# A fast matrix product with seven multiplications: the fourth product accumulates on the bank of the first, sixth and seventh

## The chip, the core and the metric

The kernel runs on one core of one Trainium2 chip. The core has a matmul engine (PE, with its weight loads shown apart as PEld), a vector engine (DVE), a scalar engine (ACT), a general engine (POOL) and a queue engine (SP) that issues most DMAs. [...] The metric is device time in microseconds: the median of several executions.

## The reference

One layer: a norm, one wide projection, two groups of attention heads, and an output projection.

```python
h = rms_norm(x, pre_g)
z = jnp.einsum('bsd,de->bse', h, w_in)
qa, ka, va, ga, qb, kb, vb, gb, gk_low = split_columns(z)
...
oa = diff_attention(qa, ka, va, lam)          # 8 heads, two softmax maps each
oa = rms_norm(oa, subln_g) * (1.0 - lam_init) * silu(ga)
...
ob = gla_chunked(qb, kb, vb, log_a)           # 4 heads of gated linear attention
ob = rms_norm(ob, gla_g) * silu(gb)
y = jnp.einsum('bse,ed->bsd', jnp.concatenate([oa, ob], axis=-1), w_out)
return x + rms_norm(y, post_g)
```

The sequence and the model width are both 1024. `z` has 7184 columns. The change concerns the product of `h` (1024 x 1024) and `w_in`.

## The kernel before

**Split numbers.** Every 32-bit number is split into a high part in a matmul format and a low part, the rest. A product a x b is made of three matmul passes: high x high, high x low, low x high. An operand therefore costs an ACT cast for the high part and a DVE subtraction for the low part. For the weights these are lines 315 and 316.

**Seven products for eight.** The columns of `w_in` are taken 256 at a time: a *pair* of 128-column blocks. For each pair the 2 x 2 block product of the input (halves of the sequence by halves of the model width) and the weights (halves of the width by the two column blocks) is made by Winograd's form of Strassen's method. With h11, h12, h21, h22 the blocks of the input, and b11 to b22 those of the weights:

- s1 = h21 + h22, s2 = s1 - h11, s3 = h11 - h21, s4 = h12 - s2
- T1 = b12 - b11, T2 = b22 - T1, T3 = b22 - b12, T4 = b21 - T2
- product 1: h11 b11; 2: h12 b21; 3: s4 b22; 4: h22 T4; 5: s1 T1; 6: s2 T2; 7: s3 T3
- result (0,0) = 1 + 2; (0,1) = 1 + 6 + 5 + 3; (1,0) = 1 + 6 + 7 + 4; (1,1) = 1 + 6 + 7 + 5

(The fourth product's sign follows from how T4 is formed.) There are 28 pairs. Eight of them, the values of the two attention groups (kinds VB and VA), are *wide*: two of them are joined to a group of 512 columns, their weights are the moving operand, and a product has 24 matmuls of 256 columns. The other 20 are single; a product has 12 matmuls of 512 columns.

**Order.** `order` (lines 200 to 221) is the list of (pair, product), 196 in all. The first ten entries are first and second products of pairs 0 to 4, which only need the first half of the sequence. PE runs the matmuls in exactly the order of the program (`mm` keeps program order); the instructions of DVE, ACT and most of SP are ordered by the program's planner when it is built, by readiness and the order of writing. `go(n)` makes n steps; each step prepares the weights up to three entries ahead (`prepare`, `make_weights`) and then does `step(i)`.

**Banks.** `take_bank` hands out the eight PSUM banks in turn from a list of free ones. In `step`, products 1, 6 and 7 accumulate on bank x, 5 and 3 on bank z, 2 on bank y, and 4 on another bank named y. `snap` copies x to SBUF on ACT after products 1, 6 and 7 (s1, s2, s3, line 427). `done` (line 436) adds a bank and a snapshot on DVE (line 440, for wide pairs lines 403 and 411) and hands the sum to `take` or `take_values`, which scale, gate or split it and store it to DRAM through SP.

**Weights.** The raw halves of `w_in` come into four buffers with the tag raw (`load_raw`, line 194), which `fetch_raw` asks for at certain products. `make_weights` forms T1 to T4 in place in those buffers on DVE (line 296, one difference at each of products 5, 6, 4 and 7), casts them on ACT and makes the low part on DVE, into a ring of five tiles.

**Input blocks.** `blocks(j)` (lines 550 to 571) makes piece j of four of h22, s1, s2 and s3 from the second half of the sequence, by PE transposes, ACT and DVE; it runs between the first ten products. s4 follows in lines 623 to 627.

**Around it.** `wo_step` (line 580) splits `w_out` on the side: it opens a load of one 128 x 512 tile at products 2 and 4 and casts, subtracts and stores it at products 1 and 6. `low_rank` and `decay` make the gates of the linear attention between the projections; from pair 12 on, `gla` puts its matmuls between the products. The last eight entries of `order` (`LEAD`) run after the first loads of the attention, mixed with loads of the split `w_out` (`weights`, line 900) into the places of the input blocks that are no longer needed; the stores of these last steps keep the program's order on SP. Behind the projections come the attention of eight heads, and the output projection, `ypart` and `yps`.

Of the kernel before, what the change touches and what calls it, by code (L numbers as in the profile page):

```python
# [31 lines left out]
def hymba_kernel(  # L32
# [188 lines left out]
    order += [(y, 7), (z, 4), (z, 7), (y, 3), (z, 3)]  # L221
# [28 lines left out]
    def fetch_raw(p, n, i):  # L250

        if not wide(p):
            load_raw(p)
            if i >= n_early:
                load_raw(p + 1)
        elif p >= 4 or p == 0:
# [4 lines left out]
            if n == 4:  # L261
                load_raw(p + 2, (0,))
                if p == 0:
                    load_raw(3, (0,))
            elif n == 7:
                if p == 0:
                    load_raw(3, (1,))
                else:
                    load_raw(p + 2, (1,))
        else:  # L270
            if n == 5:
                load_raw(2, (1,))
            elif n == 4:
                load_raw(4, (0,))
            elif n == 7:
                load_raw(4, (1,))

    def make_weights(i):
# [6 lines left out]
        else:  # L285
# [13 lines left out]
            if n == 5:  # L299
# [3 lines left out]
            elif n == 4:  # L303
                src = sub(b21, b21, b11)
            elif n == 7:
                src = sub(b12, b22, b12)
            else:
                src = {1: b11, 2: b21, 3: b22}[n]
# [40 lines left out]
    def take(kind, n, half, unit, c):  # L349

        cs = cols(half)
        if kind in ("QA", "KA"):
# [3 lines left out]
            if ending and order[made[0] - 1][1] == 7:  # L356
# [5 lines left out]
            act.activation(hi, c, AF.Copy, scale=scale)  # L362
            dve.scalar_tensor_tensor(lo, c, scale, fp(hi), ALU.mult, ALU.subtract)
# [6 lines left out]
        elif kind in ("GA", "GB"):  # L370
            g = t_st("g")
            act.activation(g, c, AF.Exp, scale=-1.0)
            act.activation(g, g, AF.Ln, bias=1.0)
            act.activation(g, g, AF.Exp, scale=-1.0)
            dve.tensor_tensor(c, c, g, ALU.mult)
            d = g_d[n + unit] if kind == "GA" else gg_d[n][unit]
            sp.dma_start(d[:, cs], c)
        elif kind == "QB":
# [3 lines left out]
            dve.scalar_tensor_tensor(c, c, QSCALE, e_q[:, cs], ALU.mult, ALU.mult)  # L382
# [8 lines left out]
        else:  # L391
            g = n + unit
            dve.tensor_tensor(c, c, decs[g][1][:, cs], ALU.mult)
            sp.dma_start(gq_d[g][2, :, cs], c)

    def take_values(p, half, unit, p0, p1):
# [1128 lines left out]
```

## Time and profile before

| what | us |
|---|---|
| median of three runs | 982.13 |
| lowest and highest of them | 981.99, 982.59 |
| the profiled execution's own time | 980.34 |
| its span, first to last instruction | 978.6 |
| granted PE clock over the span | 0.999 |
| first matmul of a projection starts | 13.96 |
| last projection ends, first output matmul starts | 630.80 |

Rows of groups read: line of the kernel, engine, operation, output <- inputs by the program's names, count; then times. In a list in order of time the first two numbers are the start and the length in us, and in brackets stands how long the engine had been idle and what ended that. Rows of stretches give the length, then the busy time of PE, PEld, DVE, ACT and POOL, the granted clock, the DMA share and GB/s. Rows of waits give who waited for whom, the total, how many times, and the longest.

### The profile page before, as it was taken

The page shows a single profiled execution, that of the slowest core. Times are in us where ns is not written, and L with a number is a line of the kernel's source. Part 1 is how long each engine was busy: PE and PEld are TensorE (multiplying, and loading weights), DVE is VectorE, ACT ScalarE, POOL GpSimd, SP SyncE. Part 2 cuts the span into 40 slices and gives each one's busy share as a digit, 9 for nine tenths or more (in the row PEclk, how much of TensorE's full clock was granted, in tenths as well). Part 3 has the DMA queues.
Part 4 walks back from the last instruction along what each step waited for, and adds up shares of the span by engine and source line. Part 5 has one row for each costly group of instructions (what it writes and reads, how often), then busy time and mean ns, then how long its engine had stood idle before and what let it go on. Part 6 is the DMA issues. An engine that isn't in the chain of part 4 may idle for free.

```text
span 978.6 us, 15745 instructions
## 1 busy us (share of the span) xinstructions
PE 956.6 (98%) x5338; PEld 829.7 (85%) x5338; DVE 736.0 (75%) x1452; ACT 600.9 (61%) x1164; POOL 135.3 (14%) x142
## 2 busy tenths in 40 slices
PE   6999999999999999999999999999999999999997
PEld 5998988888889998899888888878888888888785
DVE  6986597798766677586786876487888888898554
ACT  8642365486467445445566765366777687887773
POOL 4300000000000010000100100021322222443322
PEclk9999999999999999999999999999999999999999
DMA  9443456646765858897988866997657669994777
GB/s 353 143 123 93 124 148 202 229 169 233 253 234 168 266 183 276 247 299 230 298 254 255 270 191 217 357 300 250 206 173 234 233 202 351 351 283 107 151 209 146
DMA packets 152593, 220.45 MB, mean 225 GB/s; under 512 B 17104, under 2 KB 83664, under 8 KB 152416
## 3 DMA queue, kind: packets, MB, share of 16 engines
q1 hardware_dynamic: 148480, 212.10, 66.5%
q0 software_dynamic: 4032, 7.34, 4.8%
q8 instruction: 42, 0.69, 0.3%
q14 instruction: 39, 0.32, 0.1%
HBM read 133.93 MB, written 88.60 MB: 227 GB/s over the span
## 4 chain that ended last, share of the span: by engine, by line
PE 87%; DMA 4%; DVE 4%; ACT 2%; issue 1%; SPq 1%; POOL 0%; DVEq 0%; ACTq 0%; POOLq 0%
PE x L117 21%; PE y L117 14%; PE z L117 14%; PE ypart L117 13%; PE sc L117 7%; PE po L117 5%; PE yps L117 4%; PE wtr L120 3%; PE gpo L117 2%; DMA ks<-k_d 1%; PE kv L117 1%; DMA wo_raw<-in_w_out_dram 1%; DMA w_raw<-in_w_in_dram 1%; PE gkl_ps L117 1%; DVE w L316 1%
## 5 line engine op out<-in xcount | busy, mean ns | idle before, releaser
L315 ACT CAST w<-w_raw 128x512 fp32r<-128x512 f32 (+1 forms) x164 | 112.4, 688 | 97.2 <-PE y L117 46.2
L316 DVE TENSOR_TENSOR w<-w_raw,w 128x512 fp32r<-128x512 f32 (+1 forms) x164 | 126.5, 773 | 52.1 <-ACT w L315 45.6
L1048 ACT ACTIVATE p<-p,stt 128x896 f32<-128x896 f32 (+7 forms) x128 | 99.3, 777 | 37.7 <-DVE stt L1038 33.6
L427 ACT COPY s<-x 128x512 f32<-128x512 f32 x84 | 49.1, 585 | 86.9 <-PE x L117 83.9
L1054 POOL TENSOR_SCALAR p<-p,stt,lam 128x1024 f32<-128x1024 f32 (+3 forms) x64 | 56.2, 877 | 226.2 <-DVE stt L1053 223.8
L296 DVE TENSOR_TENSOR w_raw<-w_raw 128x512 f32<-128x512 f32 (+1 forms) x96 | 75.8, 790 | 15.4 <-DMA w_raw<-in_w_in_dram 14.1
L1038 DVE CUSTOM_DVE_ANT_0 p<-sc,maskt 128x512 f32<-128x512 f32 (+3 forms) x128 | 74.3, 585 | 14.9 <-PE sc L117 13.8
L775 POOL TENSOR_SCALAR_AFFINE_SELECT gan<-gan 128x512 f32<-128x512 f32 x8 | 17.6, 2198 | 486.3 <-ACT gan L774 486.3
L117 PE MATMUL ypart<-wo_hi,m_hi 128*128 128x512 f32 x192 | 79.6, 414 | 0.1
L117 PE MATMUL y<-h_hi,w 128*128 128x512 f32 x320 | 79.6, 391 | 0.0
L117 PE MATMUL z<-s_hi,w 128*128 128x512 f32 x320 | 79.6, 391 | 0.0
L117 PE MATMUL x<-s_hi,w 128*128 128x512 f32 x320 | 79.6, 391 | 0.0
L117 PE MATMUL ypart<-wo_hi,m_lo 128*128 128x512 f32 x192 | 75.5, 393 | 0.0
L117 PE MATMUL ypart<-wo_lo,m_hi 128*128 128x512 f32 x192 | 75.4, 393 | 0.0
L117 PE MATMUL sc<-k,q 128*128 128x512 f32 (+1 forms) x192 | 69.0, 363 | 1.2 <-DVE stt L1038 1.2
L117 PEld LDWEIGHTS x<-s_hi,w 128*128 128x128 f32 x320 | 59.7, 188 | 12.2
L117 PEld LDWEIGHTS y<-h_hi,w 128*128 128x128 f32 x320 | 59.6, 188 | 12.2
L117 PEld LDWEIGHTS z<-s_hi,w 128*128 128x128 f32 x320 | 59.5, 188 | 12.0
L117 PE MATMUL sc<-ks,q 128*128 128x512 f32 (+1 forms) x192 | 66.1, 347 | 1.0 <-DMA ks<-k_d 1.0
L1096 ACT CAST wt_hi<-wtr 128x512 fp32r<-128x512 f32 (+1 forms) x80 | 42.8, 535 | 25.3 <-PE wtr L120 24.5
L1097 DVE TENSOR_TENSOR wt_lo<-wtr,wt_hi 128x512 fp32r<-128x512 f32 (+1 forms) x80 | 50.6, 633 | 9.1 <-ACT wt_hi L1096 8.5
L1057 DVE SCALAR_TENSOR_TENSOR p<-p,stt,p 128x1024 f32<-128x1024 f32 (+3 forms) x64 | 52.1, 814 | 4.1 <-POOL p L1054 3.9
(224 smaller groups left out, 2237.3 us busy)
## 6 DMA issues: line engine op xcount, KB each, us to landing
w_raw<-in_w_in_dram SPq DMA_DIRECT2D x56, 512.0 KB, 4.5
wo_raw<-in_w_out_dram SPq DMA_DIRECT2D x32, 256.0 KB, 2.8
wo_d<-wo_hi SPq DMA_DIRECT2D x32, 256.0 KB, 2.9
wo_d<-wo_raw SPq DMA_DIRECT2D x32, 256.0 KB, 3.3
q<-q_d SPq DMA_DIRECT2D x32, 256.0 KB, 4.6
k<-k_d SPq DMA_DIRECT2D x32, 256.0 KB, 5.3
ks<-k_d SPq DMA_DIRECT2D x64, 128.0 KB, 6.5
wo_hi<-wo_d SPq DMA_DIRECT2D x16, 512.0 KB, 6.4
```

Source lines behind the costliest of these rows:

```text
L117: tc.keep_in_program_order(pe.matmul(*a, **k))
L120: tc.keep_in_program_order(pe.transpose(dst, src, ident))
L296: dve.tensor_tensor(dst, a, b, ALU.subtract)
L315: act.copy(w[0], src)
L316: dve.tensor_tensor(w[1], src, fp(w[0]), ALU.subtract)
L427: act.copy(b[k], ps)
L1038: ins = dve.tensor_tensor_reduce(p[:, a:e], sc[:, : e - a], maskt[:, NZ + P - (e - a) :] if last else maskt[:, : e - a], 1.0, 3e38 if i == ...
L1048: act.activation(p[:, :n], p[:, :n], AF.Exp, bias=st[:, m : m + 1], scale=-1.0, accum_out=st[:, 2 + m : 3 + m],)
L1054: pool.tensor_scalar(p1[:, :n], p1[:, :n], st[:, 5:6], lam, ALU.mult, ALU.mult)
L1057: dve.scalar_tensor_tensor(p0[:, :n], p0[:, :n], st[:, 4:5], p1[:, :n], ALU.mult, ALU.subtract)
L1096: act.copy(hi[:, :n], pt[:, :n])
L1097: dve.tensor_tensor(lo[:, :n], pt[:, :n], fp(hi[:, :n]), ALU.subtract)
```

## The change

Product 4 no longer takes a bank: it accumulates on x behind products 1, 6 and 7, so that the result (1,0) stands complete in PSUM, and `done` hands the bank itself on without an add. The order of a pair becomes 1, 2, 6, 5, 7, the next pair's 1, 4, 3 (for a wide group 1, 2, 6, 5, 7, 4, 3, each for both of its pairs). The swap of two entries by hand is gone. The weights' sums are formed in another order: at product 6 T3 (in b12) and T2 (in b11), at product 5 T4 (in b21) and T1, none at 7 and 4; the last two pairs keep the old way, and their order gets 7 ahead of 4. The loads of raw weights and the steps of `w_out` hang on other products.

```diff
-    for prev, group in zip([[]] + groups, groups):
-        for n in (1, 2, 5, 6, 4, 7):
-            if (group[0], n) not in order[:n_early]:
-                order += [(p, n) for p in group]
-
-            if n == (7 - len(group) if group[0] < EARLY else 2):
-                order += [(p, 3) for p in prev]
-
-    i = order.index((1, 4))
-    order[i : i + 2] = order[i + 1], order[i]
-
-    order += [(y, 1), (y, 2), (y - 1, 3), (y, 5), (z, 1), (z, 2), (z, 5), (y, 6), (z, 6), (y, 4)]
-    order += [(y, 7), (z, 4), (z, 7), (y, 3), (z, 3)]
+    for group, after in zip(groups, groups[1:] + [[y]]):
+        for n in (1, 2, 6, 5, 7, 4, 3):
+            order += [(p, n) for p in group if (p, n) not in order]
+
+            if n == 7 and len(group) == 1:
+                order += [(p, 1) for p in after[:1]]
+
+    order += [(y, 2), (y, 5), (z, 1), (z, 2), (z, 5), (y, 6), (z, 6), (y, 7)]
+    order += [(z, 7), (y, 4), (z, 4), (y, 3), (z, 3)]
...
-            if i >= n_early:
+            if i >= n_early and n > 1:
                 load_raw(p + 1)
...
-            if n == 4:
+            if n == 7:
                 load_raw(p + 2, (0,))
+            elif n == 4:
                 if p == 0:
-                    load_raw(3, (0,))
-            elif n == 7:
-                if p == 0:
-                    load_raw(3, (1,))
+                    load_raw(3)
                 else:
                     load_raw(p + 2, (1,))
         else:
-            if n == 5:
+            if n == 6:
                 load_raw(2, (1,))
+            elif n == 7:
+                load_raw(4, (0,))
             elif n == 4:
-                load_raw(4, (0,))
-            elif n == 7:
                 load_raw(4, (1,))
...
-            if n == 5:
+            if n == 5 and p < y:
+                sub(b21, b21, b11)
+                src = sub(b11, b22, b11)
+            elif n == 6 and p < y:
+                sub(b12, b22, b12)
+                dve.tensor_tensor(b11, b11, b12, ALU.add)
+                src = b11
+            elif n == 5:
                 src = sub(b11, b12, b11)
...
-    def take(kind, n, half, unit, c):
+    def take(kind, n, half, unit, src, c):
...
-            act.activation(hi, c, AF.Copy, scale=scale)
-            dve.scalar_tensor_tensor(lo, c, scale, fp(hi), ALU.mult, ALU.subtract)
+            act.activation(hi, src, AF.Copy, scale=scale)
+            dve.scalar_tensor_tensor(lo, src, scale, fp(hi), ALU.mult, ALU.subtract)
...
-            dve.tensor_tensor(st, p0, p1, ALU.add)
+            if p1 is None:
+                act.copy(st, p0)
+            else:
+                dve.tensor_tensor(st, p0, p1, ALU.add)
...
-        name = {1: "x", 2: "y", 5: "z", 6: "x", 4: "y", 7: "x", 3: "z"}[n]
-        if n in (1, 2, 4, 5):
+        name = {1: "x", 2: "y", 5: "z", 6: "x", 4: "x", 7: "x", 3: "z"}[n]
+        if n in (1, 2, 5):
             b[name], b["i" + name] = take_bank([P, 512], name)
         ps = b[name]
-        multiply(i, ps, n not in (6, 7, 3))
-
-        def done(half, unit, p0, p1):
+        multiply(i, ps, n in (1, 2, 5))
+
+        def done(half, unit, p0, p1=None):
             if wide(p):
                 return take_values(p, half, unit, p0, p1)
             c = t_c("c")
-            dve.tensor_tensor(c, p0, p1, ALU.add)
-            take(kind, m, half, unit, c)
+            if p1 is not None:
+                dve.tensor_tensor(c, p0, p1, ALU.add)
+                p0 = c
+            take(kind, m, half, unit, p0, c)
...
         elif n == 7:
             snap("s3", ps)
+            done(1, 1, b["z"], b["s3"])
+        elif n == 4:
+            done(1, 0, ps)
             free.append(b["ix"])
-            done(1, 1, b["z"], b["s3"])
-            done(1, 0, b["y"], b["s3"])
-            free.append(b["iy"])
...
-        if n in (1, 6) and wo_open:
+        if n in (3, 6) and wo_open:
...
-        if n in (2, 4) and wo_todo:
+        if n in (2, 7) and wo_todo:
...
     go(2)
     mix0 = mix(0)
-    go(3)
+    go(4)
     weights(E + 6)
     weights(E + 7)
-    go(3)
+    go(2)
```

More of the change, by code (lines that the diff above doesn't have):

```diff
@@ L355, in take @@
             ending = made[0] > len(order) - LEAD
[L356 removed]
+            if ending and order[made[0] - 1][1] in (7, 4):
                 raw = ap.tile([P, 2, 512], F32R, tag="raw", name="qk_st", bufs=4)
@@ L439, in done @@
             c = t_c("c")
-            dve.tensor_tensor(c, p0, p1, ALU.add)
-            take(kind, m, half, unit, c)
+            if p1 is not None:
+                dve.tensor_tensor(c, p0, p1, ALU.add)
+                p0 = c
+            take(kind, m, half, unit, p0, c)
         if n == 1:
```

24 lines of the change are left out of this document (13 added, 11 removed).

## The prediction

> **What bounds the kernel now.** I read the page's head and its chain of waits first, then the stage table, then the waits of the matmul engine.
>
> ```profile
> span 978.6 us, 15745 instructions
> PE 956.6 (98%) x5338; PEld 829.7 (85%) x5338; DVE 736.0 (75%) x1452; ACT 600.9 (61%) x1164; POOL 135.3 (14%) x142
> PE 87%; DMA 4%; DVE 4%; ACT 2%; issue 1%; SPq 1%; POOL 0%; DVEq 0%; ACTq 0%; POOLq 0%
> ```
>
> PE holds 87% of the chain, so only what PE waits for is worth anything. The stages (length, then PE, weight load, DVE, ACT, POOL busy):
>
> ```profile
> 20.00:64.00 44.00, 42.57 (x334) 41.12 (x333) 42.63 (x66) 30.20 (x51) 9.87 (x10) 1.00 0.50 162
> 126.00:308.00 182.00, 182.00 (x833) 151.77 (x832) 144.20 (x235) 106.17 (x182) 0.66 (x1) 1.00 0.65 211
> 308.00:478.00 170.00, 169.18 (x1187) 158.15 (x1186) 121.74 (x181) 91.28 (x156) 10.99 (x5) 1.00 0.79 247
> 478.00:609.00 131.00, 131.00 (x651) 111.08 (x651) 96.48 (x155) 83.79 (x152) 5.93 (x2) 1.00 0.76 239
> 631.00:664.00 33.00, 30.66 (x147) 24.50 (x146) 25.75 (x78) 18.32 (x42) 6.62 (x8) 1.00 0.95 308
> ```
>
> The seven-product projections run from about 14 to 631 us. From 126 to 308 and from 478 to 609 PE has no idle time at all, and DVE, the engine that the change relieves, has slack. Only 20 to 64 is different: there DVE is busy 42.63 of 44 us. What PE waits for in the whole run:
>
> ```profile
> PE xT L120 <- DVE x L482: 8.9, 4, 7.2
> PE y L117 <- DVE s L565: 1.3, 1, 1.3
> PE sc L117 <- DMA ks<-k_d: 1.0, 1, 1.0
> PE y L117 <- ACT s L427: 0.7, 1, 0.7
> PE gpo L117 <- DVE gu L803: 0.5, 1, 0.5
> PE kv L117 <- DVE c L411: 0.3, 1, 0.3
> ```
>
> Apart from the first 14 us, which the change doesn't touch, the ceiling of any gain in the projections and just behind them is 1.3 + 1.0 + 0.7 + 0.5 + 0.3 = 3.8 us, and most of these waits don't come from what the change removes. Losses have no such ceiling.
>
> **The removed adds: 0 us.** Product 4 now lands on the bank that already holds products 1, 6 and 7, so the sum for the block (1, 0) is ready in PSUM. For each of 28 pairs one DVE add of this kind goes:
>
> ```profile
> L440 DVE TENSOR_TENSOR c<-y,s x39: 678/681/692, 130.3 to 626.8; 128x512 f32<-128x512 f32 x39
> L427 ACT COPY s<-x x70: 563/589/599, 129.1 to 625.6; 128x512 f32<-128x512 f32 x70
> ```
>
> That is 28 x 0.68 = 19 us of DVE time, of which four (kind VB) come back as ACT copies of 0.59. All of it lies beside PE, which is full in these stages; without that cover it would be worth up to 19 us, but the row of 126 to 308 leaves PE nothing to win. The readers of the fourth product now read PSUM instead of SBUF; the nearest row for that (the snapshots' 0.59) is no longer than a copy from SBUF (0.62, below), so nothing is added.
>
> **The new wait on the bank: 0 us, with a bound.** Product 4 may not write before the snapshot of product 7 has been taken from the same bank. Between the two stands the next pair's product 1 (single pairs) or the other pair's product 7 (double pairs). A product of the first kind lasts 161.95 - 159.23 = 2.72 us, and here is its snapshot:
>
> ```profile
> 159.23 1.98 PE L117 MATMUL x<-s_hi,w 128*128 128x512 f32 x8
> 161.05 1.07 PE L117 MATMUL x<-s_lo,w 128*128 128x512 f32 x4
> 161.95 1.98 PE L117 MATMUL y<-h_hi,w 128*128 128x512 f32 x8
> 162.15 0.59 ACT L427 COPY s<-x 128x512 f32<-128x512 f32 x1 [2.10 <-PE x L117]
> ```
>
> The product ends at 161.05 + 1.07 = 162.12, the copy starts 0.03 later and is done 0.62 after it, with 2.1 us to spare. This is product 6 of pair 6, and product 7 follows on its bank after one product, just as 6, 5, 7 and 7, 1, 4 will stand; the old kernel does this all along without a wait. So I take 0. Where it fails is when ACT, whose queue is in order, is held up by something ahead of the snapshot. It happens once in a large way:
>
> ```profile
> 514.22 2.07 PE L117 MATMUL x<-s_hi,w 128*128 128x512 f32 x8
> 517.03 1.98 PE L117 MATMUL y<-h_hi,w 128*128 128x512 f32 x8
> 520.66 0.62 ACT L584 CAST wo_hi<-wo_raw 128x512 fp32r<-128x512 f32 x1 [7.33 <-DMA wo_raw<-in_w_out_dram]
> 521.19 0.58 ACT L427 COPY s<-x 128x512 f32<-128x512 f32 x1
> 522.79 2.07 PE L117 MATMUL x<-s_hi,w 128*128 128x512 f32 x8
> ```
>
> ACT waited 7.33 us for a load of the output weights; the snapshot of product 6 (PE 514.22) ended at 521.77 and the next product on that bank started at 522.79, only because other matmuls stood between. With a single 2.72 us product between, it would be due at 517.03 + 2.72 = 519.75, so PE would lose 2.0 us. The change also moves these loads: opened with product 2 and used with 6, one product later, where three lay between. Waits of this kind are 27.8 us in 15 pieces:
>
> ```profile
> ACT wo_hi L584 <- DMA wo_raw<-in_w_out_dram: 27.8, 15, 7.3
> ```
>
> The lower bound is 0; the upper is four pieces of 2.0, 8 us. I take 0, as the old distance of 6 to 7 never cost anything, and keep 8 for a rival.
>
> [...]
>
> **The bank count: -0.7 us.** Product 4 takes no bank of its own. The wait of 0.7 on ACT's snapshot is the early product 4 of pair 1 which found all eight banks taken (five first products, two fifths, one fourth). It is gone.
>
> **The order 6 before 5 in the first double pair: +4.6 us.** This is the largest term. The blocks s1 (for product 5) and s2 (for 6) of the input are being built on DVE and ACT just then. The rows around it:
>
> ```profile
> 46.24 0.74 DVE L565 SCALAR_TENSOR_TENSOR s<-xT,pre_g,h 128x512 f32<-128x512 f32 x1
> 51.64 1.22 DVE L296 TENSOR_TENSOR w_raw<-w_raw 128x1024 f32<-128x1024 f32 x1
> 53.38 0.68 DVE L569 TENSOR_TENSOR f1hi<-s,f1hi 128x512 f32<-128x512 f32 x1
> 54.09 0.62 ACT L547 CAST s_hi<-f1hi 128x512 fp32r<-128x512 f32 x1 [0.15 <-DVE f1hi L569]
> 55.78 1.21 DVE L296 TENSOR_TENSOR w_raw<-w_raw 128x1024 f32<-128x1024 f32 x1
> 58.66 0.68 DVE L548 TENSOR_TENSOR s_lo<-f1hi,s_hi 128x512 fp32r<-128x512 f32 x1
> 51.21 2.08 PE L117 MATMUL z<-w,s_hi 128*128 128x256 f32 x16
> 54.08 2.08 PE L117 MATMUL z<-w,s_hi 128*128 128x256 f32 x16
> 56.96 2.45 PE L117 MATMUL x<-w,s_hi 128*128 128x256 f32 x16
> 60.20 2.08 PE L117 MATMUL x<-w,s_hi 128*128 128x256 f32 x16
> ```
>
> Today product 5 of pairs 0 and 1 starts at 51.21 and 54.08, product 6 at 56.96; s2's last piece (row 53.38, cast at 54.09, low part at 58.66) is complete at 59.34, just ahead of its use. With 6 first, s2 is due at 51.21. The last low piece serves only the last two of 24 matmuls, 0.24 us at 2.88 / 24 each, so the first product can't end before 59.34 + 0.24 = 59.6, where without a wait it ends at 54.08: a loss of 5.5. Today's product 6 lasts 60.20 - 56.96 = 3.24 instead of 2.88, a loss of 0.36 that goes. Net 5.15.
>
> Can s2 come earlier? The weights' four differences stay four, but T4 = b21 - T2 moves ahead, out of the place at 55.78 to some time after T2; if an idle moment of DVE takes it, all behind it come 1.2 earlier and the loss is 5.15 - 1.2 = 4.0. If it sits in the full stretch, nothing is won and the loss stays 5.15. I take the middle, 4.6. The bounds lie wider. The chain alone would need 46.98 + 0.68 + 0.62 + 0.68 = 48.96, before 51.21: if DVE served s2 first, nothing is lost and 0.36 won. If DVE's fill grows by one more difference, 5.15 + 1.2 = 6.3. The diff says nothing on DVE's order, which the program's planner sets from readiness, and today readiness puts differences and weight casts ahead of s2's pieces; none of that is altered before the point in question. What is late next: nothing, I think. After a stall of 5 us PE asks for the following weights and blocks that much later, while DVE goes on.
>
> **Loads of the raw weights: 0 us.** The next pair's load is asked for at product 2 instead of 1, since the buffers come free only after 4 and 3.
>
> ```profile
> w_raw<-in_w_in_dram SPq DMA_DIRECT2D x56, 512.0 KB, 4.5
> ```
>
> A load lands in 4.5 us and is used four products, 4 x 2.72 = 10.9 us, later. The differences for 6 come as two in a row on DVE, each about as long as the add above (0.68), and are prepared three products ahead; if that cover went, the second would cost 0.7 us a pair.
>
> **The end of the projections: -0.5 us.** SP's stores of the last two pairs are in program order:
>
> ```profile
> 622.13 4.93 SPq L367 DMA_DIRECT2D k_d<-qk_st  x8
> 629.22 7.10 SPq L367 DMA_DIRECT2D q_d<-qk_st  x8
> 643.03 1.06 SPq L989 DMA_DIRECT2D v<-v_d  x2
> ```
>
> They come in lumps of eight until 643, and the loads of values, mixes and head 1's keys queue behind them. With 7, 7, 4, 4 they start a product earlier and in fours, with the four loads of output weights behind sixteen instead of eight. Between nothing and the whole wait of 1.0 for ks goes; half.
>
> **Sum.** +4.6 - 0.7 - 0.5 = +3.4. The profiled execution took 980.34 us, so it would take 983.7; the median of the runs, 982.13, lies 1.8 above it, so I forecast 982.13 + 3.4 = **985.5**.
>
> **The rivals.** *s2 is in time* (28%): DVE's order follows the need. Then -0.36 - 0.7 - 1.0 = -2.1, 980.0, and 979.2 if the two waits of 0.8 in the middle go as well. For it: the chain of 48.96; against it: DVE busy 42.63 of 44. *ACT late at a snapshot* (15%): a load of output weights blocks ACT ahead of the snapshots of 6 or 7, three times 2.0 with 0.7 won back, 982.13 + 5.3 = 987.4; it decides once ACT is held for over 2.1 us behind a product 6 or 7. For it: the wait of 7.33; against: no such loss in the old kernel, and it needs an accident of place. *Nothing that PE sees* (7%): adds and order both vanish under PE, 982.1. My forecast has 50%, its own range 983.8 to 987.
>
> Faster or slower here means by over 0.2%, 1.96 us, about what a measurement tells from no change. The forecast is slower but for 3 of its 50 points; of the first rival 20 points are faster and 8 the same; of the third 5 same and 2 faster. So faster 0.22, same 0.16, slower 0.62. The range runs from 979.2 (first rival) to 989.0 (forecast with 6.3, or the second rival with one more piece).
>
> **What would show it.** Right: in the new trace the first product on s2 starts near 51 and lasts some 8 us, held by s2's last low piece near 59; no wait of PE on ACT's snapshot at 69; no waits from 126 to 609. Wrong: PE goes through 51 to 60 without a gap, since s2's last piece comes before 52; or gaps ahead of a fourth or seventh product, ended by an ACT copy.

## The result, and the profile after

The changed kernel is slower: 995.92 us (median of four runs, 992.88 to 1000.32) against 982.36 for the kernel before in the same session; the ratio is 1.0144 with an interval of 1.0113 to 1.0175. The forecast was 985.5, with a range up to 989.0. The profiled execution is the longest of the four, 1000.32 us, so the two profiles lie 20.0 us apart and the medians 13.6; why single runs of this kernel differ that much is taken up in the last section and stays open.

The head of the page and its chain of waits, after:

```profile
span 998.6 us, 15706 instructions
PE 965.0 (97%) x5338; PEld 833.2 (83%) x5338; DVE 716.8 (72%) x1424; ACT 606.5 (61%) x1168; POOL 132.8 (13%) x142
PE 75%; DMA 10%; DVE 7%; issue 3%; ACT 3%; SPq 1%; POOL 0%; DVEq 0%; ACTq 0%; POOLq 0%
```

DVE's work shrank from 736.0 to 716.8 us, as the change meant. But PE's share of the chain fell from 87% to 75%, and that of DMA rose from 4% to 10%: PE now waits for things that wait for transfers. The stage table (length, then PE, weight load, DVE, ACT, POOL busy, clock, DMA share, GB/s):

```profile
20.00:64.00 44.00, 37.87 (x273) 36.26 (x272) 40.87 (x64) 28.44 (x49) 11.38 (x10) 0.92 0.47 151
126.00:308.00 182.00, 177.47 (x789) 144.99 (x788) 135.77 (x223) 101.05 (x175) 0.63 (x1) 1.00 0.60 194
308.00:478.00 170.00, 170.00 (x1195) 159.21 (x1194) 116.25 (x171) 93.74 (x155) 8.84 (x4) 1.00 0.78 245
478.00:609.00 131.00, 128.40 (x639) 107.89 (x638) 89.13 (x145) 82.65 (x148) 4.32 (x3) 0.99 0.75 235
55.00:60.00 5.00, 2.14 (x10) 2.14 (x11) 5.00 (x9) 3.04 (x4) 0.00 (x0) 0.69 0.09 20
60.00:65.00 5.00, 5.00 (x30) 5.00 (x30) 3.91 (x8) 2.66 (x5) 0.00 (x0) 0.63 0.67 190
```

Both stages in which PE had been full now have holes (4.5 and 2.6 us), and in the stretch from 55 to 65 the granted clock itself is low (0.69 and 0.63), where the old kernel has 1.00 from 20 to 976 us. What PE waits for, the largest rows that the old kernel doesn't have:

```profile
PE x L117 <- ACT s L436: 4.4, 4, 1.6
PE x L117 <- ACT s_hi L558: 3.4, 1, 3.4
PE xT L120 <- POOL xt L493: 1.4, 1, 1.4
...
PE gms L117 <- DVE sq_hl L846: 1.3, 1, 1.3
PE gms L117 <- ACT sq_hl L845: 0.6, 1, 0.6
```

(`gms` is a matmul of the linear attention's norm.) The four waits for an ACT snapshot (L436) stand ahead of fourth products. And two queues are held by transfers more than before:

```profile
DVE w_raw L290 <- DMA w_raw<-in_w_in_dram: 43.8, 15, 7.1
ACT wo_hi L595 <- DMA wo_raw<-in_w_out_dram: 39.3, 14, 7.2
```

The second row stood at 27.8 in the kernel before. The first, which the prediction never looked at, was this:

```profile
DVE w_raw L296 <- DMA w_raw<-in_w_in_dram: 14.1, 9, 3.6
```

To see where the time goes, the start of the 37th product and of the last of the 196 products is compared with the old kernel (134.8 and 628.1 us); up to either mark both kernels have done the same products, in another order. The changed kernel is 8.1 us late at the first mark and 19.0 at the second: 8.1 us are lost ahead of it, around the first double pairs, and 11.0 behind it. All experiments are measured on this scale too. In the expectations that follow, (5,4) stands for product 4 of pair 5, and the 34.6 and 13.7 us that DVE is said to wait for raw weights, in the changed kernel and the one before, are counted from 126 to 650 us.

**The early 8 us.** PE, DVE and ACT rows in order of time; first PE, then DVE, then ACT:

```profile
31.88 0.76 PE L120 MATMUL xT<-ident,xt 128*128 128x128 f32 x5 [1.45 <-POOL xt L493]
...
53.62 0.87 PE L117 MATMUL x<-w,s_hi 128*128 128x256 f32 x6
57.86 2.50 PE L117 MATMUL x<-w,s_hi 128*128 128x256 f32 x10 [3.37 <-ACT s_hi L558]
60.16 1.91 PE L117 MATMUL x<-w,s_lo 128*128 128x256 f32 x8
```

```profile
26.36 1.21 DVE L290 TENSOR_TENSOR w_raw<-w_raw 128x1024 f32<-128x1024 f32 x1
27.49 0.15 DVE L1500 SCALAR_TENSOR_TENSOR ssq<-ssq 128x2 f32<-128x2 f32 x1
...
55.77 0.70 DVE L580 TENSOR_TENSOR f1hi<-s,f1hi 128x512 f32<-128x512 f32 x1
59.91 0.70 DVE L559 TENSOR_TENSOR s_lo<-f1hi,s_hi 128x512 fp32r<-128x512 f32 x1
```

```profile
57.19 0.61 ACT L558 CAST s_hi<-f1hi 128x512 fp32r<-128x512 f32 x1
```

The first product on s2 starts at 53.62 and stops after six matmuls, since s2's last piece (DVE 55.77) is cast only at 57.19. Two more things belong to it: at 26.36 one of the new weight differences stands on DVE ahead of the last step of a norm (27.49), and PE waits 1.45 for the block that hangs on it; and from 56.92 to 63.74, from inside the gap on, the granted clock is at 0.50 for 6.8 us (the two stretches from 55 to 65 above: 0.69 and 0.63).

**The later 11 us.** The four waits ahead of fourth products have several holders. Ahead of (5,4) it is an activation of a decay, which waits 4.13 us for DVE; ahead of (9,4) a row of gates and decays that ACT works off almost without a wait; ahead of (11,4) and (12,4) casts of output weights, before which ACT is idle for 6.21 and 7.21 us. The last of them, ACT and PE:

```profile
296.89 0.62 ACT L595 CAST wo_hi<-wo_raw 128x512 fp32r<-128x512 f32 x1 [7.21 <-DMA wo_raw<-in_w_out_dram]
297.42 0.61 ACT L316 CAST w<-w_raw 128x512 fp32r<-128x512 f32 x1
297.94 0.58 ACT L436 COPY s<-x 128x512 f32<-128x512 f32 x1
```

```profile
298.56 1.67 PE L117 MATMUL x<-h_hi,w 128*128 128x512 f32 x6 [1.25 <-ACT s L436]
```

Another place shows what a load can do at the head of DVE's queue. DVE, ACT and PE rows around 542:

```profile
541.81 0.69 DVE L290 TENSOR_TENSOR w_raw<-w_raw 128x512 f32<-128x512 f32 x1 [2.10 <-DMA w_raw<-in_w_in_dram]
542.42 0.68 DVE L450 TENSOR_TENSOR c<-z,s 128x512 f32<-128x512 f32 x1
```

```profile
543.14 0.63 ACT L374 ACTIVATE g<-c 128x512 f32<-128x512 f32 x1 [4.06 <-DVE c L450]
543.68 0.57 ACT L436 COPY s<-x 128x512 f32<-128x512 f32 x1
```

```profile
543.16 2.11 PE L117 MATMUL z<-s_hi,w 128*128 128x512 f32 x8 [0.23 <-DVE c L450]
```

At the head of DVE's queue stands a difference of raw weights, which waits 2.10 us for its load and starts at 541.81. The add on bank z starts only behind it, at 542.42, PE's third product waits for that add, ACT's gate (L374) waits for it too, and a snapshot stands behind the gate. PE loses only 0.23 us here; the place shows the chain and not the size.

### The profile page after: what moved, and what is told of

It reads as the page before. It is cut to its first block, busy times and chain, and to the rows that moved or that the text cites. A ratio compares the mean times of both kernels' runs of the same rounds, so it can differ in the third digit from the quotient of the medians.

```text
span 998.6 us, 15706 instructions
## 1 busy us (share of the span) xinstructions
PE 965.0 (97%) x5338; PEld 833.2 (83%) x5338; DVE 716.8 (72%) x1424; ACT 606.5 (61%) x1168; POOL 132.8 (13%) x142
## 4 chain that ended last, share of the span: by engine, by line
PE 75%; DMA 10%; DVE 7%; issue 3%; ACT 3%; SPq 1%; POOL 0%; DVEq 0%; ACTq 0%; POOLq 0%
PE x L117 22%; PE ypart L117 12%; PE z L117 12%; PE sc L117 6%; PE po L117 5%; PE y L117 5%; PE yps L117 4%; DMA wo_d<-wo_raw 3%; PE wtr L120 3%; PE gpo L117 2%; DMA wo_raw<-in_w_out_dram 2%; DMA w_raw<-in_w_in_dram 2%; DMA ks<-k_d 1%; DVE w L317 1%; PE kv L117 1%
## 5 line engine op out<-in xcount | busy, mean ns | idle before, releaser
L316 ACT CAST w<-w_raw 128x512 fp32r<-128x512 f32 (+1 forms) x164 | 111.6, 686 | 76.9 <-PE z L117 23.1
L290 DVE TENSOR_TENSOR w_raw<-w_raw 128x512 f32<-128x512 f32 (+1 forms) x74 | 57.2, 776 | 47.7 <-DMA w_raw<-in_w_in_dram 43.8
L117 PE MATMUL x<-h_hi,w 128*128 128x512 f32 x320 | 80.5, 393 | 4.5 <-ACT s L436 4.4
L436 ACT COPY s<-x 128x512 f32<-128x512 f32 x84 | 48.9, 582 | 57.5 <-PE x L117 56.2
L786 POOL TENSOR_SCALAR_AFFINE_SELECT gan<-gan 128x512 f32<-128x512 f32 x8 | 13.8, 1724 | 507.0 <-DVE w_raw L290 255.1
L117 PE MATMUL z<-s_hi,w 128*128 128x512 f32 x320 | 80.6, 394 | 0.2 <-DVE c L450 0.2
L117 PE MATMUL x<-s_hi,w 128*128 128x512 f32 x320 | 79.9, 392 | 0.0
L117 PE MATMUL ypart<-wo_hi,m_hi 128*128 128x512 f32 x192 | 79.5, 414 | 0.1
L117 PE MATMUL ypart<-wo_hi,m_lo 128*128 128x512 f32 x192 | 75.5, 393 | 0.0
L117 PE MATMUL ypart<-wo_lo,m_hi 128*128 128x512 f32 x192 | 75.4, 393 | 0.0
L117 PEld LDWEIGHTS x<-h_hi,w 128*128 128x128 f32 x320 | 59.1, 188 | 18.7 <-ACT s L436 7.0
L117 PEld LDWEIGHTS z<-s_hi,w 128*128 128x128 f32 x320 | 60.0, 189 | 13.2 <-DVE c L450 0.9
L117 PE MATMUL sc<-k,q 128*128 128x512 f32 (+1 forms) x192 | 68.9, 363 | 2.0 <-DVE stt L1049 1.4
L117 PEld LDWEIGHTS x<-s_hi,w 128*128 128x128 f32 x320 | 59.7, 188 | 12.9 <-ACT s L436 0.7
L117 PE MATMUL sc<-ks,q 128*128 128x512 f32 (+1 forms) x192 | 66.1, 348 | 0.5 <-DMA ks<-k_d 0.5
```

Source lines behind the costliest of these rows:

```text
L117: tc.keep_in_program_order(pe.matmul(*a, **k))
L290: dve.tensor_tensor(dst, a, b, ALU.subtract)
L316: act.copy(w[0], src)
L436: act.copy(b[k], ps)
```

## The experiments

The table gives for each kernel the median, the ratio to the kernel before in the same session with its interval, and the lateness of the 37th product and what is added to it until the last. In brackets stands the 95% interval. Lateness is read from one profiled run of each kernel, and that run need not lie at the median (e14's is the longest of its ten). The old kernel's median in the five sessions lay between 980.4 and 981.5.

| kernel | median us | ratio | late at product 37 | added by the last |
|---|---|---|---|---|
| the changed kernel | 995.9 | 1.0144 [1.0113, 1.0175] | 8.1 | 11.0 |
| e1_wo_spaced | 997.6 | 1.0164 [1.0149, 1.0180] | 7.5 | 10.9 |
| e2_early_old | 992.3 | 1.0121 [1.0100, 1.0142] | 0.3 | 11.7 |
| e3_both | 989.5 | 1.0088 [1.0073, 1.0103] | 0.2 | 8.7 |
| e4_before_early | 987.2 | 1.0079 [1.0051, 1.0106] | 7.2 | -0.4 |
| e5_cover | 990.6 | 1.0100 [1.0082, 1.0119] | 0.9 | 10.3 |
| e6_decay | 988.7 | 1.0073 [1.0052, 1.0094] | 1.1 | 8.6 |
| e7_own_bank | 1001.3 | 1.0207 [1.0189, 1.0225] | 7.2 | 13.1 |
| e8_own_bank_e3 | 990.0 | 1.0088 [1.0069, 1.0107] | 4.3 | 7.0 |
| e9_before_nudge | 980.9 | 1.0001 [0.9987, 1.0016] | 0.3 | 0.8 |
| e10_before_late_sums | 998.2 | 1.0179 [1.0134, 1.0223] | 1.0 | 16.2 |
| e11_old_sums | 1006.8 | 1.0255 [1.0236, 1.0273] | 2.0 | 23.1 |
| e12_late_t3 | 998.1 | 1.0164 [1.0138, 1.0190] | 10.1 | 8.8 |
| e13_late_t3_e3 | 984.5 | 1.0035 [1.0021, 1.0048] | 0.5 | 5.4 |
| e14_late_t3_e10 | 984.8 | 1.0042 [1.0022, 1.0062] | 0.7 | 7.2 |
| e15_late_t3_e5 | 983.7 | 1.0025 [1.0011, 1.0040] | 0.4 | 2.9 |
| e16_both_held | 998.0 | 1.0167 [1.0148, 1.0187] | 10.2 | 10.1 |
| e17_best | 983.7 | 1.0021 [1.0010, 1.0032] | 1.0 | 2.1 |
| e18_before_wo | 980.0 | 0.9990 [0.9977, 1.0002] | -0.2 | -1.0 |

### First round: the early part, and the output weights

e4 puts the order 6 before 5 and the new sums into the old kernel, for the first double pair alone:

```diff
-        for n in (1, 2, 5, 6, 4, 7):
+        for n in (1, 2, 6, 5, 4, 7) if group[0] == 0 else (1, 2, 5, 6, 4, 7):
...
+            if p == 0 and n == 5:
+                sub(b21, b21, b11)
+                src = sub(b11, b22, b11)
+            elif p == 0 and n == 6:
+                sub(b12, b22, b12)
+                dve.tensor_tensor(b11, b11, b12, ALU.add)
+                src = b11
...
```

> The kernel before, with the first wide group alone (pairs 0 and 1) in the order 6 before 5 with the new weight sums; nothing else of the change. Theory 'early order': the whole early loss appears by itself, 7 to 8 us, so 989 to 990. If it needs the other parts of the change, under 3 us: 982 to 985.

e2 is the reverse, the changed kernel with the old order, sums and raw loads for pairs 0 to 3. e1 gives each load of an output-weight tile more time, and e3 does both:

```diff
-        if n in (3, 6) and wo_open:
+        if n in (2, 7) and wo_open:
...
-        for n in (1, 2, 6, 5, 7, 4, 3):
+        for n in (1, 2, 5, 6, 7, 4, 3) if group[0] < 4 else (1, 2, 6, 5, 7, 4, 3):
...
-            if n == 5 and p < y:
+            new = 4 <= p < y
+            if n == 5 and new:
...
-            elif n == 6 and p < y:
+            elif n == 6 and new:
```

> The changed kernel, but a tile of the output weights is now cast where the next one is opened, at products 2 and 7, so that three or four products lie between its load and its use instead of one at every second tile. Theory 'held ACT' (the cast waits for its load at the head of ACT's queue, the snapshot of product 7 stands behind it, and product 4 waits for that snapshot): ACT's waits for these loads fall from 39 us to under 20, the waits of PE on the snapshot from 4.4 us to under 1.5, and the time from 995.9 to 990 to 992. Theory 'one product is too little cover': PE still waits 4 us on the snapshots, and the time stays within 2 us of 995.9.

> The changed kernel, but the four pairs of the first two wide groups keep the old order of 5 before 6 and the old weight sums; their fourth product still accumulates. Theory 'early order' (s2 is not built yet when product 6 comes first, and three differences at once delay the norms): the lag of 8 us that the changed kernel has at its twelfth product is gone, and the time falls by 7 to 8, to 988 to 989. Theory 'the loss is spread over the projections and would come up elsewhere': under 3 us is won, since PE then runs ahead and waits later.

> Both edits together. If the two causes are separate and make up the loss, the gains add up: 7.5 and 5, so 982.5 to 985, near the old kernel. If a third cause matters (raw weights that land late for the two differences of product 6: DVE waited 34.6 us for them in the changed kernel, 13.7 before), some 3 to 5 us stay: 986 to 989.

e4 has the same gap of 3.37 at the same place, is 7.2 us late behind it and stays so: the early loss is shown by itself, 5.7 us by the medians. e2 has it gone, but wins only 3.6 us by the medians, where 7 to 8 were expected. And e1 gains nothing, though ACT's waits ahead of casts of output weights fall from 39.3 to 17.7 us: the losses behind product 37 moved to other places and stayed 10.9, while DVE's waits for raw weights rose from 43.8 to 60.8 us. In e3 the largest single one has another holder. ACT, then PE:

```profile
149.57 1.06 ACT L718 ACTIVATE t<-b 128x1024 f32<-128x1024 f32 x1 [4.14 <-DVE b L711]
150.53 0.57 ACT L436 COPY s<-x 128x512 f32<-128x512 f32 x1
```

```profile
151.15 3.65 PE L117 MATMUL x<-h_hi,w 128*128 128x512 f32 x8 [2.45 <-ACT s L436]
```

An activation of a decay holds ACT for 4.14 us, waiting for DVE, with the snapshot of product 7 behind it; product 4 waits, and its eight matmuls then last 3.65 instead of 1.98 us.

### Second round: cover, the decay, the bank

e5 puts two products between 7 and 4, e6 writes the second decay later, both on top of e3:

```diff
+                if after[0] == y or not wide(after[0]):
+                    order += [(after[0], 2)]
...
-            if i >= n_early and n > 1:
+            if i >= n_early and n > 2:
```

```diff
-    go(7)
+    go(11)
     decay(1)
```

e7 undoes the accumulation alone in the changed kernel, e8 the same in e3:

```diff
-        name = {1: "x", 2: "y", 5: "z", 6: "x", 4: "x", 7: "x", 3: "z"}[n]
-        if n in (1, 2, 5):
+        name = {1: "x", 2: "y", 5: "z", 6: "x", 4: "y", 7: "x", 3: "z"}[n]
+        if n in (1, 2, 4, 5):
...
-            done(1, 0, ps)
-            free.append(b["ix"])
+            done(1, 0, ps, b["s3"])
+            free.append(b["iy"])
```

> The changed kernel with the old order and old sums for pairs 0 to 3 and the output-weight tiles spaced (as in e3_both), and for single pairs one more product between the seventh and the fourth: 7, next 1, next 2, 4, 3; the raw weights of the next pair are asked for at product 6 instead of 2. Theory (one product of 2.72 us is too little cover for the snapshot of product 7, and for the add that empties bank z): in e3_both the snapshot of (5,7) was done at 151.10 and PE had been ready for (5,4) at 148.70; with 2.72 more it is ready at 151.42, so the gap of 2.45 and the half-clock stretch behind it go, 4.3 us, and the z wait of 1.07 near 272 goes too; 989.5 - 5.4 = 984.1, and down to 982.6 if the 1.48 before a product near 548 goes with them. Rival (the loss is not a matter of cover, but of work moved on DVE and ACT): the waits come back elsewhere, 987.5 to 990.

> e3_both with the second decay written four products later, behind product 7 of pair 5 instead of ahead of it, so that its activations, which wait for DVE, no longer stand ahead of that snapshot in ACT's queue. Theory (an activation waiting for DVE at the head of ACT's queue is what makes the snapshot late): the gap at 151 and the half clock behind it go, 4.3 us: 985.2, later stretches as in e3_both. Rival (removing one hold-up only lets PE run into the next): a gap of 1 to 3 us before a product 7 or 4 a pair later, 987 to 989.

> The changed kernel as it is, with one part undone: product 4 again opens a bank of its own, and the block (1,0) is again the sum of that bank and the snapshot of product 7 on DVE; order, weights' sums, loads and output weights stay those of the changed kernel. Theory (the one bank is what puts the snapshot of 7 on PE's path): no wait of PE on an ACT snapshot ahead of a fourth product (in the changed kernel 1.58, .73, .08, .87 and 1.25, together 4.5), DVE back near 736 us, the 8 us before 70 unchanged, the z waits and those in the last projections unchanged or a little longer: 990 to 993. Rival (the order, the weights' sums and the loads alone do it): 995 to 998. Second rival (the removed adds did help somewhere): over 996, with new waits of PE on DVE.

> The same undone in e3_both: product 4 with its own bank, in the new order 7, next 1, 4, 3. Theory: the gap of 2.45 at 151 and its half-clock stretch go, 4.3 us; the z wait of 1.07 and the losses after 509 (gms .77 and .66, 1.48) stay in part: 989.5 - 4.3 = 985.2, and 983.5 if the 1.48 goes too. Rival (order and loads, not the bank): 988 to 990.

The theory of this round fell. In e5 and e6 the wait that was aimed at is gone, the one near 151, and others come in its place: in e5 ahead of *seventh* products (1.08 at 222, 3.37 at 245), in e6 ahead of seventh and third ones. In e7 no fourth product waits any more and DVE is back at its old work, yet the kernel is slower than the changed one, by 5.4 us by the medians (1.6 by the profiles):

```profile
PE 964.2 (96%) x5338; PEld 832.0 (83%) x5338; DVE 735.5 (74%) x1452; ACT 601.8 (60%) x1164; POOL 131.4 (13%) x142
...
DVE w_raw L290 <- DMA w_raw<-in_w_in_dram: 43.6, 17, 7.1
```

So the shared bank decides where the loss shows, not that there is one. What did not change between the changed kernel and e7 is the second row. The second rival of e7's expectation fits too: PE waits 3.9 us for DVE's adds on bank z, against 0.2 in the changed kernel, so the removed adds seem to be worth something where DVE is held. Beside e3 the bank makes no difference by the medians: e8 loses 4.1 us ahead of product 37, where PE waits 2.1 for a weight of the low-rank gates, and 1.7 less than e3 behind.

### Third round: the old kernel nudged, and the sums

e9 only moves decays 0 and 2 by a product (`go(9)` to `go(10)`, `go(2)` to `go(3)`). e10 is the counterpart of e4: the old kernel with 6 before 5 and the new sums from pair 4 on. e11 is e3 with the old sums and the order 5, 6, 7, next 1, 4, 3 for all pairs:

```diff
-        for n in (1, 2, 5, 6, 4, 7):
+        for n in (1, 2, 5, 6, 4, 7) if group[0] < 4 else (1, 2, 6, 5, 4, 7):
...
-            if n == 5:
+            new = 4 <= p < y
+            if new and n == 5:
+                sub(b21, b21, b11)
+                src = sub(b11, b22, b11)
+            elif new and n == 6:
+                sub(b12, b22, b12)
+                dve.tensor_tensor(b11, b11, b12, ALU.add)
+                src = b11
...
```

```diff
-        for n in (1, 2, 5, 6, 7, 4, 3) if group[0] < 4 else (1, 2, 6, 5, 7, 4, 3):
+        for n in (1, 2, 5, 6, 7, 4, 3) if True else ():
...
-            new = 4 <= p < y
+            new = False
```

> The kernel before with nothing of the change in it; only decays 0 and 2 are written one product later (the same work, the same order of products). Theory A (the fixed order that the planner gives ACT and DVE is what keeps the old kernel free of waits, and any edit deals it anew): new waits of PE of 1 to 3 us on an ACT snapshot or on a DVE add, 983 to 987. Theory B (it is the order of the changed kernel, one product between 7 and 4 and the new sums, that makes the waits): none of them, 980 to 982.

> The kernel before with the new sums and product 6 ahead of 5 from pair 4 on, except the last two; pairs 0 to 3 and everything else are old. Theory A: 983 to 987, with waits at places of its own. Theory B, the sums at fault (two differences in a row on DVE ahead of product 6): 984 to 988, with PE waiting for weights or for snapshots behind them from 126 on; the bank at fault: 980 to 982, as product 6's snapshot now even has two products of cover.

> e3_both with the old order 5, 6 and the old sums for all pairs, so that the one bank, the order 7, next 1, 4, 3, the raw loads at product 2 and the output-weight places are what is left of the change. Theory A: again 985 to 990, the waits at other places than in e3_both. Theory B, the bank and its order at fault: 988 to 990 with the gap before (5,4) near 151; the sums at fault: 981 to 984.

Theory A fell: the old kernel bears a nudge without a new wait. e10 was the surprise: 17 us from the sums and the order of 5 and 6 alone, with the banks, the loads and the output weights all as they were. Its DVE row, and one of six such places on DVE and PE:

```profile
DVE w_raw L296 <- DMA w_raw<-in_w_in_dram: 64.4, 19, 7.2
```

```profile
257.83 0.69 DVE L296 TENSOR_TENSOR w_raw<-w_raw 128x512 f32<-128x512 f32 x1 [3.77 <-DMA w_raw<-in_w_in_dram]
258.44 0.68 DVE L450 TENSOR_TENSOR c<-z,s 128x512 f32<-128x512 f32 x1
```

```profile
259.18 2.11 PE L117 MATMUL z<-s_hi,w 128*128 128x512 f32 x8 [0.82 <-DVE c L450]
...
282.88 1.30 PE L117 MATMUL x<-s_hi,w 128*128 128x512 f32 x5
```

One of the new sums in each pair is an addition with a line of its own (L305), so the differences can be counted off by pairs: the one at 257.83 is T3 = b22 - b12 of pair 12, whose product 6 starts at 282.88. DVE waits 3.77 us for a load of pair 12's weights, whose first product starts only at 272.92, to form a difference that is used 25 us later. The adds of pair 10 wait behind it: both inputs of the one at 258.44 had been ready since 253.56, when the snapshot of (10,7) was done. The reason is in the code. The old first difference, T1, is written into b11, and product 1's weights have to be made from b11 before. T3 is written into b12, which no plain product reads. So it may stand right behind its load, and there the planner, which goes by readiness, puts it; on the chip the load comes later than that. Counted the same way, the T3s of single pairs for which DVE waits in the changed kernel stand, from pair 5 on, 26 to 38 us ahead of their products (the one at 541.81 is that of pair 24, whose product 6 starts at 575.04).

e11 tells something else: with product 7 right behind product 6 there is nothing to hide the snapshot, and each pair pays for it.

```profile
PE x L117 <- ACT s L436: 18.2, 17, 5.2
...
207.77 1.43 PE L117 MATMUL x<-s_hi,w 128*128 128x512 f32 x5 [0.68 <-ACT s L436]
```

The bare price is 0.68 us, and fourteen of the seventeen waits are of this size. So e11's time can't say what the old sums are worth; it says why the change has to put 6 ahead of 5. Its wait of DVE for raw weights does agree with T3 as the holder: 11.1 us with the old sums, against 44.4 in e3.

### Fourth round: the difference held back

An edge is an order of two instructions that the planner has to keep. Here it is one edge on DVE's order, with no instruction added: T3 may not stand ahead of the low part of the weights of the entry before.

```diff
+    last_w = []
...
-                sub(b12, b22, b12)
+                with tc.issue_after(last_w[-1].ins):
+                    sub(b12, b22, b12)
...
-        dve.tensor_tensor(w[1], src, fp(w[0]), ALU.subtract)
+        last_w.append(dve.tensor_tensor(w[1], src, fp(w[0]), ALU.subtract))
```

It goes into the changed kernel (e12), e3 (e13), e10 (e14) and e5 (e15).

> The changed kernel with one edge added and nothing else: the difference b22 - b12 of product 6 may not stand on DVE ahead of the low part of the weights of the entry before (p, 6). Theory (that difference, put into DVE's queue right behind its raw load and 20 us ahead of its use, holds DVE and all adds and casts behind it): DVE's waits for raw loads fall from 34.6 to under 12, the waits of PE from 126 to 609 on ACT snapshots, z adds and gms fall from about 9 to under 3, the early 8 us stay: 988 to 991. Rival (bank and cover): unchanged, 995 to 998.

> e3_both (old order and sums for pairs 0 to 3, output weights spaced) with the same edge. Theory: the 4.3 us at 151, the z wait of 1.07 and most of the 3 us after 509 go: 981 to 985. Rival (bank and cover): 988 to 990.

> The kernel before with the new sums and 6 ahead of 5 from pair 4 on (e10, 998.2) and the same edge. Theory: DVE's waits for raw loads fall from 64.4 to under 20, the six z waits (6.9 us) go and the 2.95 before (23,6) too: 981 to 985. Rival (two differences in a row ahead of product 6, wherever they stand, are the cost): 992 to 998.

> e5_cover (two products between 7 and 4) with the same edge. Theory: as e13 or better, as nothing of one product's cover is left at 4: 980 to 984. Rival (cover doesn't matter once DVE isn't held): the same as e13 within 1 us.

In e14 DVE's wait falls from 64.4 to

```profile
DVE w_raw L297 <- DMA w_raw<-in_w_in_dram: 8.9, 5, 3.8
```

and the time from 998.2 to 984.8; not one product waits for a z add any more. e13 and e15 gain 5.1 and 7.0 us. With DVE free, cover seems to count: e15 adds 2.9 us behind product 37 where e13 adds 5.4, though their medians can't be told apart. In e12 the row is gone altogether, and yet the kernel is no faster; the expectation was missed. Product by product e12 and the changed kernel can be set side by side, since their order is the same: behind 300 us the changed kernel loses 5.5 us that e12 doesn't, all of them between 520 and 560, so the edge is worth that much there. But ahead of 300 us e12 loses more. The early loss grew by 2 us (the norm step is in time now, but PE waits 6.5 us instead of 3.4 for s2's high pieces). Behind product 37, 8.8 us are left of 11.0, all of them ahead of 300 us. ACT and PE at the largest of these:

```profile
280.34 0.62 ACT L597 CAST wo_hi<-wo_raw 128x512 fp32r<-128x512 f32 x1 [7.86 <-DMA wo_raw<-in_w_out_dram]
280.86 0.61 ACT L318 CAST w<-w_raw 128x512 fp32r<-128x512 f32 x1
281.38 0.58 ACT L438 COPY s<-x 128x512 f32<-128x512 f32 x1
```

```profile
282.01 2.48 PE L117 MATMUL x<-h_hi,w 128*128 128x512 f32 x5 [2.52 <-ACT s L438]
```

Here the holder is the cast of an output-weight tile. e12 and e13 have the same order of products from pair 4 on and the same edge; what differs there is the place of these loads, and e13 waits for them much less:

```profile
ACT wo_hi L597 <- DMA wo_raw<-in_w_out_dram: 10.8, 4, 5.8
```

It adds 5.4 us where e12 adds 8.8. So by these two profiles spacing the loads is worth 3.4 us, though e12 and e13 also differ in pairs 0 to 3. While DVE was held, it was worth nothing in the changed kernel (e1) and 2.7 us by the medians from e2 to e3; that DVE alone decides it is not shown.

### Fifth round: the casts of output weights held back

```diff
+    last_a = []
...
-        act.copy(w[0], src)
+        last_a.append(act.copy(w[0], src))
...
-            act.copy(hi, raw)
+            with tc.issue_after(last_a[-1].ins):
+                act.copy(hi, raw)
```

Here `last_a[-1]` is the newest cast of projection weights. e16 is e12 with it, e17 e15, e18 the kernel before.

> e12 (the changed kernel with the difference held back) with one more edge: the cast of an output-weight tile may not stand on ACT ahead of the newest weight cast written before it. Theory (those casts, waiting for their loads, are the second holder): ACT's waits before wo_hi fall from 35.6 to under 12 and the gaps ahead of fourth products with them; the early 8 to 10 us stay: 988 to 992. Rival (the order with one product between 7 and 4 is the cost by itself): 995 to 998.

> e15 (old order and sums for pairs 0 to 3, two products between 7 and 4, the difference held back) with the same edge on the casts of output weights. Theory: the 2.16 and the half-clock stretch near 242 go, and what DVE and ACT no longer carry is not worth anything to PE: 979 to 981.5, no more than 1.5 below the kernel before. Rival (another hold-up takes the place): 983 to 985.

> The kernel before with the same edge on the casts of output weights alone. Theory: ACT's waits there fall from 27.8 to under 12, and PE, which waits for none of them, gains nothing: 980 to 982. Rival: a new wait appears, 983 to 986.

The edge did not bite. In e16 ACT still waits:

```profile
ACT wo_hi L599 <- DMA wo_raw<-in_w_out_dram: 42.9, 13, 7.6
```

So e16 doesn't test the second holder, and what is known of it is the comparison of e12 and e13. e17 stays 2 us above the kernel before, with a last gap of 2.6 ahead of a seventh product near 243, the same place as the 2.16 in e15. e18 can't be told from the kernel before. None of these kernels beats it.

## Why the prediction was wrong

The direction was right; the size was 3.4 us where the medians differ by 13.6 and the profiles by 20.0.

- **The step that failed** is "Loads of the raw weights: 0 us", where it says that the differences for product 6 "are prepared three products ahead". That is where the program writes them, not where the planner puts them. In the changed kernel T3 stands 26 to 38 us ahead in the single pairs from 5 on, at the head of DVE's queue with its load outstanding; in place of 0, or 0.7 a pair, holding it back is worth 13.4 us in e14, 7.0 in e15 and 5.1 in e13. In the changed kernel by itself (e12) it wins 5.5 us behind 300 us and loses as much ahead of it. The prediction's own row for the load (4.5 us, used 10.9 later) was right about the product and didn't ask what else waits for the load.
- **The new wait on the bank, 0**: right for the bank itself, since a bank of its own wins nothing (e7, e8), and e11 gives the bare price that one product hides, 0.68 against the 0.62 in which the copy of the prediction's rows was done. "No waits from 126 to 609" was wrong. The row named as a sign of error, gaps ahead of a fourth product ended by an ACT copy, did come, four times, 4.4 us together: within the bound of 8 that was given there, and not the 0 that went into the sum.
- **The rival "ACT late at a snapshot"** (15%, 987.4) named a true mechanism and saw it as an accident of place worth 5.3. It needed no accident: ACT is held by loads of output weights, by decays that wait for DVE and by its own gates. DVE's hold by T3 stands behind none of the four waits ahead of fourth products; it shows in waits for z adds (0.2 us here, 6.9 in e10) and in the 5.5 us behind 300 us that e12 doesn't lose.
- **The order 6 before 5, +4.6**: right in kind and nearly in size. s2's last low piece is done at 59.91 + 0.70, against the 59.34 forecast, and in e7, where the ten matmuls behind the gap of 3.37 last 1.46 us instead of 2.50, the step costs 4.5, or 4.1 less the 0.36 that goes. But it is the cast of s2's last high piece, at 57.19, that PE waits for, and not the low piece as forecast. Left out were the norm step behind a new difference, 2.4 us late, and the half clock (6.8 us in the changed kernel, 3.4 in e4). Together they make 8.1 in the changed kernel's profile, 7.2 in e4's, and 5.7 by e4's medians.
- **The bank count, -0.7**: right; the lateness falls by 0.8 at that place and the wait is gone.
- **The removed adds, 0**: right beside a DVE that has slack. DVE lost 19.2 us of work, against 19 forecast, and with DVE no longer held e15 and e17 still don't pass the old kernel. Where DVE is held it may be otherwise (e7).
- **The end, -0.5**: the sign was wrong. The wait for ks fell from 1.0 to 0.5, but the last matmuls of the attention that wait (`po`, weights by values) come 0.9 us later relative to the last projection (start at 927.48 before and 947.43 after, 19.95 later, against 19.0). Two waits of PE behind the projections are new, 0.6 and 0.4 us, both for DVE. The list of PE's waits in the prediction also leaves out the row "PE sc L117 <- DVE stt L1038: 1.2, 2, 0.9", which lies just behind the projections, so the ceiling of 3.8 should be 5.0.

The sum of the shown parts, by medians: 995.9 to 992.3 without the early part, 989.5 with the output weights spaced too, 984.5 with T3 held back, 983.7 with more cover. The old kernel's own median moves from 982.4 to 980.8 over these sessions; by the ratios the parts are 2.3, 3.2, 5.2 and 1.0 us, and 2.5 remain. The step to more cover is within the spread. Much of what remains may be the gap near 243, ahead of which ACT stands idle for 4.05 us in e15 before a cast of an output-weight tile (the profile doesn't say what ended that); that it alone is the rest was not shown.

## What to carry to other kernels

An in-place sum is held back by the readers of the buffer that it overwrites, and a reordering that frees it of them lets it move up to its load and hold its engine there, as DVE stood 3.77 us for a T3 in e10 with an add behind it whose inputs had been ready for over 4 us: for each instruction of a new form, ask what is the earliest place it may take, not where it is written. When several holders stand one behind the other in the engines' queues, undoing one of them may show nothing (e1, e6 and e12 all missed), so read first who stands at the head of each queue and for what, and remove the holders together. In this kernel a product that follows on its own bank cost 0.68 us where no other product stood between (e11); by an estimate from two rows of the kernel before, the cover of one product is used up by a hold of ACT above about 2 us (2.72 for the product less 0.62 for the copy).

## What the hardware showed

After some gaps of PE the granted clock is at 0.50 for a while, and full again. In the changed kernel's profile this comes twice before the last matmuls: from 56.92 to 63.74 us, 6.8 us long, at the gap of 3.37 ahead of s2, and from 555.26 to 558.68, 3.4 us long, behind two waits for `gms` of 0.63 and 1.26 us, whose ends lie 1.75 us apart. The gaps of 1.58 and 1.25 ahead of fourth products, at 158 and 299, draw none. The kernel before, whose gaps behind the first 20 us lie apart and are at most 1.32 us, has 1.00 from there to 976 us; e9 has 0.998 over its whole run. And the same gap of 3.37 us ahead of s2 drew 6.8 us of half clock in the changed kernel and 3.4 in e4 (0.85 from 55 to 60 and 0.81 from 60 to 65), while in e7 the ten matmuls behind it last only 1.46 us, against 2.50 in the changed kernel and 2.02 in e4. Behind a gap of 2.16 in e15 eight matmuls last 2.92 instead of 1.98 us; e17, with a gap of 2.6, has 0.999 over its whole run. So the matmuls behind a gap may last longer and cost time on top of it, as also in e3 (eight in 3.65 instead of 1.98 us); what decides whether the clock falls, and for how long, was not shown. That the same gap draws different stretches may be part of the spread of the changed kernel: its longest run (1000.32) has the lowest granted clock, 0.993, and the others 0.996 (997.33), 0.997 (994.51) and 0.996 (992.88). It can't be the whole of it, since the last three differ by 4.5 us at nearly one clock, and 23 runs of the kernel before in the last session, all at 0.998 or 0.999, lie between 978.53 and 983.98.
